# Modulation sums of two feature chunks: from TensorE to VectorE, with the other sums of the stage at new places

## The chip, the core and the metric

The kernel runs on one core of one Trainium2 chip. The metric is device time in microseconds (us) of one execution; a run's number is the median of three. The core's engines are TensorE (PE; its weight loads appear as PEld), VectorE (DVE), ScalarE (ACT), GpSimd (POOL) and SyncE (SP, which here only issues DMAs). Each works through its own queue in order and waits on semaphores for the others.

## What is computed

Two encoder layers over a sequence of 256 rows and 1024 features. What matters here is that the modulation of layer l depends on the vector c alone, so that it can be computed at any time before that layer starts:

```python
c_act = silu(c)
for l in range(2):
    shift, scale, gate = split(c_act @ w_ada[l] + b_ada[l], 3)
    h = rms_norm(x, pre_norm_g[l]) * (1 + scale) + shift
    proj = h @ w_in[l]            # q k v g_att | u b c g_conv
    att = dilated_attention(q, k, v, rel_bias) * silu(g_att)
    cnv = b * short_conv(c * u, conv_w[l]) * silu(g_conv)
    x = x + gate * rms_norm(concat(att, cnv) @ w_out[l], post_norm_g[l])
```

## The kernel before

The feature dimension is cut into 8 chunks of 128. Large products are made exact by splitting each fp32 operand into a high part (`hi`, a ScalarE cast) and a rest (`lo`, a VectorE subtraction), and multiplying three times (`mm3`, lines 270 to 272).

**The main stage of the first layer** is a loop over 24 units (j = 0 to 23, line 816): `UNITS` names 12 column blocks (u0 u1 c0 c1 b0 b1 a1 g0 g1 o0 o1 o2), two units each. Units 0 to 17 are projections, 18 to 23 the start of the output product. Around each unit's matmuls stand, in the order of the code: the PE steps of attention, `scores` of head h at unit 2+2h, its `softmax` in the same unit, `divide` a unit later, `turn` (four transposes, line 596) two units later, `take` (every second head) three units later; the split of the weights that are used four units later (`AHEAD`); and the steps that `PLAN` lists for the unit. PE, ACT, DVE and POOL run in exactly the order in which the code is written (`MANUAL`), so `PLAN` is a hand-written schedule. In it `<` steps come before the unit's attention steps, `=` and `+` steps after the split, `>` steps after the matmuls.

**The modulation of the second layer** is made inside this stage, as two columns per chunk, shift and scale. There are two ways:

- *On PE* (`sums`, `cols`; chunks in `MODS_PE`, a pair at a time): `mods_sums` (line 658) multiplies two 1 MB weight blocks by the replicated silu(c), 16 small fp32 matmuls (line 312), ACT copies the result (line 317); a unit later `mods_cols` folds it with two matmuls (line 331) and three tiny DVE instructions (lines 665 to 667).
- *On DVE* (`shift`, `scale`; a chunk at a time): with the block transposed on the host, each is one dot product over the free dimension, 128x1024, with a read of its accumulator (`dot`, line 299). A chunk is two dots and one 1 MB block, named d0 to d5 here.

Before, chunks 4 and 5 (`s2`) and 6 and 7 (`s3`) are made on PE, chunks 0 to 3 (d0 to d3) on DVE. The gate sums r0 and r1 go over PE too.

**Loads.** `LOADS` is the order of SP's queue: 1 MB blocks (`s` and `r` names are two blocks) into a ring of six `raw` buffers. `load_more` issues a block once the one six places ahead of it has been consumed in the code, and on the chip its DMA waits for that reader.

**The end of the stage.** After unit 23 come the last products of the first half of the sequence (o3), their squares (ACT, line 215), the gated product `og` (DVE, line 869), `rstd` (POOL, lines 221 to 227), the new x (DVE, line 874), `xhat` and its transposes on PE (line 894), which feed the second layer.

Of the kernel before, what the change touches and what calls it, by code (L numbers as in the profile page):

```python
# [33 lines left out]


UNITS = ("u0 u1 c0 c1 b0 b1 a1 g0 g1 o0 o1 o2", "q0 k0 q1 k1 u0 u1 c0 c1 b0 b1 a0 a1 g0 g1 o0 o1 o2")
LOADS = ("u1 c0 c1 b0 r0 d0 b1 s2 a1 r1 g0 s3 g1 d1 d2 o0 o1 o2 d3 o3", "q0 k0 q1 k1 u0 u1 e0 c0 c1 e1 b0 b1 a0 a1 g0 g1 o0 o1 o2 o3")
HEAD_AT = ((2, 4, 6, 8, 10, 12, 14, 16), (6, 8, 11, 13, 16, 18, 21, 23))
PLAN = ({-1: "=heads0", 0: "=heads1", 3: "=heads2", 5: "=heads3", 6: "<gate0 +shift0", 7: "+scale0", 8: "<sums2 =taps0 =line0",
# [6 lines left out]
COLS = {"q": 0, "k": AW, "a": 3 * AW, "u": 4 * AW, "b": 4 * AW + CW, "c": 4 * AW + 2 * CW, "g": 4 * AW + 3 * CW}  # L46

ADA_PE = (0, 1)
MODS_PE = (2, 3)
LAST_ORDER = "g v store q0 k0 q1 k1"  # L50
OUT_K = (0, 4, 6, 2)
ROW_ORDER = "q0 q1 sums k0 cols k1 g v"
# [26 lines left out]
def ada_layout(w_ada):  # L79


    def by_input(l, cols):
        return [w_ada[l][:, a:b].reshape(KC, P, b - a).transpose(1, 0, 2).reshape(P, -1) for a, b in cols]

    def by_feature(l, starts):
        return np.concatenate([w_ada[l][:, a:a + P].T for a in starts], axis=1)
# [8 lines left out]
    for s in range(4):  # L95
        a = 2 * s * P
        blocks[1] += (by_input(1, ((a, a + WC), (D + a, D + a + WC))) if s in MODS_PE
                      else [by_feature(1, (a + j * P, D + a + j * P)) for j in range(2)])
# [29 lines left out]
def encoder_kernel(ctx, tc, x, w_ada, b_ada, w_row, w_cols, w_out, post_g, vecs, bias, out):  # L128
# [277 lines left out]
    for l in range(DEPTH):  # L406
# [283 lines left out]
        def load_more():  # L690

            while todo and all(n < 6 or n - 6 in consumed for n in range(len(loaded), len(loaded) + (2 if todo[0][0] in "sr" else 1))):
                load(todo.pop(0))
# [17 lines left out]
        def split_unit(name, m, late=False):  # L711

            if name[0] == "o":
                src, shape = raws[name][:, m, :], [P, D]
            elif (name, m) not in parts_of:
                src, shape = raws[name][:, :, m * P:(m + 1) * P], [P, KC, P]
            else:
                return lambda: None
            hi, lo = parts_of[name, m] = [wp.tile(shape, F32R, name=n, bufs=6) for n in ("hi", "lo")]
            nc.scalar.copy(hi, src)  # L720

            def second():
                nc.vector.tensor_sub(lo, src, hi.bitcast(F32))  # L723
                if m:
                    consumed.update(load_no[name])

            return second if late else second()
# [77 lines left out]
        if l == 0:  # L805
            for m, w in enumerate(w_u):
                parts_of["u0", m] = w
        todo = LOADS[l].split()
        load_more()
        o_ps = None  # L810
        for j in range(AHEAD):
            split_unit(*splits[j])
        for what in PLAN[l].get(-1, "").split():
            does[what[1:-1]](int(what[-1]))
        load_more()
        for j, (name, m) in enumerate(units):
            stage = {j - at: h for h, at in enumerate(HEAD_AT[l])}
            late = PLAN[l].get(j, "").split()
            for what in [w for w in late if w[0] == "<"]:
# [155 lines left out]
```

## Time and profile before

| What | Value |
|---|---|
| median of 3 runs | 293.22 us (293.03 to 293.94) |
| the profiled execution | 293.09 us, span 291.3 us |
| PE busy | 279.3 us, 96% of the span |
| DVE busy | 210.5 us, 72% |
| ACT busy | 176.0 us, 60% |
| granted TensorE clock, mean | 0.993 of full speed |

The span runs from the first to the last instruction; 1.8 us of the execution lie around it. The shares are averages: a stage in which PE never waits and a stage in which it waits for a chain over ACT, DVE and POOL stand in the same number. The main stage of the first layer lies at about 56 to 144 us of the span, the passage to the second layer at 144 to 166 us, the second layer behind it. In a row of the timeline the first number is the start in us, the second the duration in us; brackets give the time that the engine stood idle before the instruction, and who released it. Instructions of one engine overlap a little, so a step is read from start to start.

### The profile page before, as it was taken

The numbers are of one execution on the slowest core, as the hardware profiler recorded it, in microseconds if no ns is written. First come the engines' busy times: TensorE is split into PE (matmuls) and PEld (weight loads), VectorE is DVE, ScalarE is ACT, GpSimd is POOL, SyncE is SP. The second block draws the span as 40 slices with busy tenths as digits, with TensorE's granted clock in tenths as the row PEclk, the third lists the DMA queues.
The fourth block names the chain that finished last, engine by engine and source line by source line (L and its number), as shares of the span: only waits on it lengthen the run. The fifth ranks groups of instructions, "written<-read, shape, count | busy, mean of one in ns | idle before, by whom it ended". The sixth has DMA issues, their size and how long they took to land.

```text
span 291.3 us, 5502 instructions
## 1 busy us (share of the span) xinstructions
PE 279.3 (96%) x2213; PEld 252.7 (87%) x2213; DVE 210.5 (72%) x371; ACT 176.0 (60%) x318; POOL 20.7 (7%) x43
## 2 busy tenths in 40 slices
PE   7999999999999999999999899999999999999991
PEld 5868999999879879987786899999999999998880
DVE  3649999797785767769889895667887865468234
ACT  4556464999746545576366773957856655946121
POOL 2122000000000000000034400000002000000011
PEclk9999999999999999999999999999999999999997
DMA  7999999998499989755754888445477441000012
GB/s 275 415 422 415 412 403 401 414 427 334 142 389 411 378 324 373 255 197 198 281 234 145 339 313 313 168 150 204 168 251 268 150 155 61 2 0 2 1 72 73
DMA packets 12342, 72.35 MB, mean 248 GB/s; under 512 B 1635, under 2 KB 2921, under 8 KB 5020
## 3 DMA queue, kind: packets, MB, share of 16 engines
q1 hardware_dynamic: 11264, 70.39, 62.3%
q0 software_dynamic: 576, 1.09, 1.1%
q10 hardware_dynamic: 476, 0.52, 0.5%
q8 instruction: 17, 0.28, 0.4%
q14 instruction: 9, 0.07, 0.1%
HBM read 70.92 MB, written 1.07 MB: 247 GB/s over the span
## 4 chain that ended last, share of the span: by engine, by line
PE 84%; ACT 6%; DVE 6%; DMA 1%; issue 1%; POOL 1%; DVEq 0%; ACTq 0%; POOLq 0%
PE pm L270 21%; PE pm L271 21%; PE pm L272 21%; PE pm L312 3%; PE ps L604 2%; PE ps L596 2%; DVE lo L723 2%; PE ps L272 2%; PE ps L270 2%; PE ps L271 2%; PE ps L567 2%; DMA vt<-in_vecs 1%; ACT hi L720 1%; PE ps L568 1%; PE ps L414 1%
## 5 line engine op out<-in xcount | busy, mean ns | idle before, releaser
L270 PE MATMUL pm<-hT_hi,hi 128*128 128x256 f32 x408 | 116.1, 284 | 0.8 <-ACT hT_hi L498 0.8
L271 PE MATMUL pm<-hT_lo,hi 128*128 128x256 f32 x408 | 114.0, 279 | 0.1
L272 PE MATMUL pm<-hT_hi,lo 128*128 128x256 f32 x408 | 113.9, 279 | 0.0
L723 DVE TENSOR_TENSOR lo<-raw,hi 128x1024 fp32r<-128x1024 f32 x60 | 72.9, 1223 | 37.4 <-ACT hi L720 37.3
L270 PEld LDWEIGHTS pm<-hT_hi,hi 128*128 128x128 f32 x408 | 76.7, 188 | 3.4 <-issue 2.0
L271 PEld LDWEIGHTS pm<-hT_lo,hi 128*128 128x128 f32 x408 | 76.8, 188 | 0.5 <-DVE hT_lo L500 0.3
L272 PEld LDWEIGHTS pm<-hT_hi,lo 128*128 128x128 f32 x408 | 76.7, 188 | 0.0
L720 ACT CAST hi<-raw 128x1024 fp32r<-128x1024 f32 x60 | 62.3, 1048 | 5.0 <-PE pm L271 4.7
L443 DVE TENSOR_TENSOR lo<-raw,hi 128x1024 fp32r<-128x1024 f32 (+1 forms) x16 | 17.4, 1087 | 1.4 <-ACT hi L441 1.4
L270 PE MATMUL pm<-hi,hT_hi 128*128 128x256 f32 (+1 forms) x50 | 16.9, 337 | 0.5 <-DVE hT_hi L263 0.5
L580 ACT ACTIVATE prob<-prob,mx 128x256 f32<-128x256 f32 x32 | 16.0, 504 | 2.1 <-DVE mx L577 2.0
L271 PE MATMUL pm<-lo,hT_hi 128*128 128x256 f32 (+1 forms) x50 | 16.7, 334 | 0.6 <-DVE lo L723 0.6
L598 ACT COPY pT<-ps 128x512 f32<-128x512 f32 x16 | 9.4, 587 | 12.2 <-PE ps L596 12.2
L272 PE MATMUL pm<-hi,hT_lo 128*128 128x256 f32 (+1 forms) x50 | 16.7, 334 | 0.0
L577 DVE CUSTOM_DVE_ANT_0 prob<-ps,u 128x256 f32<-128x256 f32 x32 | 12.2, 420 | 5.5 <-PE ps L568 5.3
L589 ACT ACTIVATE prob<-prob,rc 128x256 f32<-128x256 f32 x16 | 8.2, 512 | 12.9 <-DVE rc L587 12.9
L441 ACT CAST hi<-raw 128x1024 fp32r<-128x1024 f32 (+1 forms) x16 | 14.3, 938 | 1.7 <-DMA raw<-in_w_row 1.7
L215 ACT ACTIVATE junk<-pm 128x512 f32<-128x512 f32 (+1 forms) x9 | 5.0, 550 | 16.6 <-PE pm L272 9.6
L299 DVE CUSTOM_DVE_ANT_0 raw<-raw,c_row,scale_g 128x1024 f32<-128x1024 f32 x10 | 13.4, 1342 | 0.0
L270 PE MATMUL pm<-hi,mix_a 128*128 128x512 f32 (+1 forms) x36 | 13.3, 370 | 0.0
L271 PE MATMUL pm<-lo,mix_a 128*128 128x512 f32 (+1 forms) x36 | 13.3, 370 | 0.0
L272 PE MATMUL pm<-hi,mix_a 128*128 128x512 f32 (+1 forms) x36 | 13.3, 370 | 0.0
(185 smaller groups left out, 473.3 us busy)
## 6 DMA issues: line engine op xcount, KB each, us to landing
raw<-in_w_cols SPq DMA_DIRECT2D x25, 1024.0 KB, 6.6
raw<-in_w_ada SPq DMA_DIRECT2D x24, 1024.0 KB, 8.0
raw<-in_w_out SPq DMA_DIRECT2D x8, 1024.0 KB, 4.8
raw<-in_w_row SPq DMA_DIRECT2D x7, 896.0 KB, 7.5
u<-t_dr SPq DMA_DIRECT2D x1, 1536.0 KB, 11.0
x_sb<-in_x SPq DMA_DIRECT2D x2, 512.0 KB, 4.5
gg<-r_dr POOLq DMA_DIRECT2D x2, 512.0 KB, 4.7
raw<-in_w_row SPq DMA_DIRECT2D x1, 512.0 KB, 7.8
```

Source lines behind the costliest of these rows:

```text
L270: nc.tensor.matmul(o, ah, bh, start=first, stop=False, **kw)
L271: nc.tensor.matmul(o, ah, bl, start=False, stop=False, **kw)
L272: return nc.tensor.matmul(o, al, bh, start=False, stop=last, **kw)
L299: nc.vector.tensor_tensor_reduce(w, w, c_row, scale=factor, scalar=first, op0=ALU.mult, op1=ALU.add, accum_out=o)
L312: nc.tensor.matmul(g_ps[32 * j:32 * j + 32, :], c_rep[:, kk + kh * (KC // 2), :], raws[t][:, kk + kh * (KC // 2), :], start=kk == 0, stop= ...
L441: nc.scalar.copy(hi, src)
L443: nc.vector.tensor_sub(lo, src, hi.bitcast(F32))
L577: nc.vector.tensor_tensor_reduce(pr_sb[:, t, :], s_ps[:, t, :], u[:, h, t * P:t * P + S][:, ::-1], scale=-1.0, scalar=3.0e38, op0=ALU.add, ...
L580: nc.scalar.activation(pr_sb[:, t, :], pr_sb[:, t, :], AF.Exp, scale=-1.0, bias=mx[:, t:t + 1], accum_out=sm[:, t:t + 1])
L598: nc.scalar.copy(pT[h], t_ps)
L720: nc.scalar.copy(hi, src)
L723: nc.vector.tensor_sub(lo, src, hi.bitcast(F32))
```

## The change

Chunks 4 and 5 leave `MODS_PE`. Their two weight blocks, of the same size, are laid out by feature, and become d4 and d5. In `PLAN` of the first layer `sums2` and `cols2` are gone, and four dots come in; nearly all dots stand at other units:

| Chunk | Before: shift, scale at unit | After |
|---|---|---|
| 0 | 6, 7 | 2, 4 |
| 4 | on PE: sums 8, cols 9 | 6, 7 |
| 1 | 13, 14 | 13, 14 |
| 2 | 16, 19 | 15, 16 |
| 5 | on PE, with 4 | 19, 21 |
| 3 | 20, 21 | 22, 23 |

`LOADS` follows: d0 goes from behind r0 to ahead of b0, d4 and d5 stand where they are needed, d3 comes last. The second layer's plan is the same.

```diff
-LOADS = ("u1 c0 c1 b0 r0 d0 b1 s2 a1 r1 g0 s3 g1 d1 d2 o0 o1 o2 d3 o3", ...
+LOADS = ("u1 c0 c1 d0 b0 r0 b1 d4 a1 r1 g0 s3 g1 d1 d2 o0 o1 o2 d5 o3 d3", ...
...
-         15: "+early0", 16: "+shift2", 17: "+side1 +sg0 >sg1 >turn0 >turn1", 18: "=conv0 =whole0", 19: "=conv1 +scale2", 20: "=att1 +shift3", 21: "+scale3"},
+         15: "+early0 +shift2", 16: "+scale2", 17: "+side1 +sg0 >sg1 >turn0 >turn1", 18: "=conv0 =whole0", 19: "=conv1 +shift5",
+         20: "=att1", 21: "+scale5", 22: "+shift3", 23: "+scale3"},
...
-MODS_PE = (2, 3)
+MODS_PE = (3,)
```

The file has one line more, so line numbers of after are higher by one. In the rows below a dot is two rows, one that reads a `raw` tile and `c_row`, and one that reads the accumulator into a column of B (shift) or A (scale).

DVE in units 2 and 3, before: the rest of a weight split, then the divide of head 0 (`rc`, `prob`).

```order
L723 TENSOR_TENSOR lo_809<-raw_715,hi_808 128x1024
L587 RECIPROCAL rc_844<-sm_813 128x2
L588 TENSOR_SCALAR prob_811<-prob_811,rc_844 128x256
L723 TENSOR_TENSOR lo_849<-raw_715,hi_848 128x1024
L399 SCALAR_TENSOR_TENSOR q_even_663<-pm_233,q_even_663 64x512
```

And after:

```order
L724 TENSOR_TENSOR lo_809<-raw_715,hi_808 128x1024
L300 ISA raw_717,B1_112<-raw_717,c_row_105,vt_89 128x1024
L300 ISA B1_112 128x1
L588 RECIPROCAL rc_845<-sm_813 128x2
L589 TENSOR_SCALAR prob_811<-prob_811,rc_845 128x256
L724 TENSOR_TENSOR lo_850<-raw_715,hi_849 128x1024
L400 SCALAR_TENSOR_TENSOR q_even_663<-pm_233,q_even_663 64x512
```

The shift dot of chunk 0 now stands ahead of the divide of head 0.

DVE in units 15 and 16, before: the gated first half of attention (`att`, `att_a`), then the softmax of the last head.

```order
L723 TENSOR_TENSOR lo_1510<-raw_1302,hi_1509 128x1024
L646 TENSOR_TENSOR att_666<-att_666,sg0_242 128x512
L648 TENSOR_TENSOR att_a_1513<-att_666,att_a_1513 128x512
L577 ISA prob_1556,mx_1557<-ps_1541,u_106 128x256
L577 ISA mx_1557 128x1
```

And after:

```order
L724 TENSOR_TENSOR lo_1485<-raw_1277,hi_1484 128x1024
L647 TENSOR_TENSOR att_666<-att_666,sg0_242 128x512
L649 TENSOR_TENSOR att_a_1488<-att_666,att_a_1488 128x512
L300 ISA raw_1233,B1_112<-raw_1233,c_row_105,vt_89 128x1024
L300 ISA B1_112 128x1
L578 ISA prob_1532,mx_1533<-ps_1517,u_106 128x256
L578 ISA mx_1533 128x1
```

The shift dot of chunk 2 now stands ahead of that softmax; its scale dot takes the old place of the shift dot, behind the softmax and the next split.

DVE from unit 20 on, before: the two splits of o3, the second half of attention, two dots of chunk 3, the first gated product.

```order
L723 TENSOR_TENSOR lo_1686<-raw_1472,hi_1685 128x1024
L646 TENSOR_TENSOR att_666<-att_666,sga_1598 128x512
L648 TENSOR_TENSOR hT_lo_108<-att_666,hT_hi_107 128x512
L299 ISA raw_1422,B1_112<-raw_1422,c_row_105,vt_89 128x1024
L299 ISA B1_112 128x1
L723 TENSOR_TENSOR lo_1700<-raw_1472,hi_1699 128x1024
L299 ISA raw_1422,A1_111<-raw_1422,c_row_105,scale_g_103,vt_89 128x1024
L299 ISA A1_111 128x1
L869 TENSOR_TENSOR og_1730<-pm_1644,gg_1642 128x512
```

And after:

```order
L724 TENSOR_TENSOR lo_1664<-raw_1447,hi_1663 128x1024
L647 TENSOR_TENSOR att_666<-att_666,sga_1576 128x512
L649 TENSOR_TENSOR hT_lo_108<-att_666,hT_hi_107 128x512
L724 TENSOR_TENSOR lo_1677<-raw_1447,hi_1676 128x1024
L300 ISA raw_1397,A1_111<-raw_1397,c_row_105,scale_g_103,vt_89 128x1024
L300 ISA A1_111 128x1
L300 ISA raw_1541,B1_112<-raw_1541,c_row_105,vt_89 128x1024
L300 ISA B1_112 128x1
L300 ISA raw_1541,A1_111<-raw_1541,c_row_105,scale_g_103,vt_89 128x1024
L300 ISA A1_111 128x1
L870 TENSOR_TENSOR og_1709<-pm_1622,gg_1620 128x512
```

No dot stands between the two splits of o3 any more; three stand behind them, directly ahead of the first gated product.

## Rows read from the trace of the kernel before

**Rows 1.** Page, part 4: the chain that ended last, shares by engine.

```profile
PE 84%; ACT 6%; DVE 6%; DMA 1%; issue 1%; POOL 1%; DVEq 0%; ACTq 0%; POOLq 0%
```

**Rows 2.** Busy time in three stretches; columns are named in the first row.

```profile
core 0: us, PE busy (x) PEld busy (x) DVE busy (x) ACT busy (x) POOL busy (x), PEclk, DMA share, GB/s
53.10:69.20 16.10, 16.10 (x135) 15.87 (x134) 13.29 (x21) 15.25 (x25) 0.00 (x0) 1.00 1.01 419
69.20:85.10 15.90, 15.90 (x152) 14.04 (x150) 12.30 (x24) 12.03 (x24) 0.00 (x0) 1.00 0.67 255
...
127.90:143.10 15.20, 14.23 (x66) 10.37 (x64) 12.17 (x16) 9.53 (x14) 0.00 (x0) 1.00 0.56 208
```

**Rows 3.** PE in order of time, around sums and columns: start, duration, instruction.

```profile
84.77 0.28 PE L271 MATMUL pm<-hT_lo,hi 128*128 128x256 f32 x1
84.89 0.27 PE L272 MATMUL pm<-hT_hi,lo 128*128 128x256 f32 x1
85.09 1.93 PE L312 MATMUL pm<-raw,c_rep 128*32 128x256 f32 x32
...
87.18 0.28 PE L568 MATMUL ps<-k_low,q_odd 128*128 128x256 f32 x1
...
90.67 0.28 PE L272 MATMUL pm<-hT_hi,lo 128*128 128x256 f32 x1
...
91.36 0.28 PE L271 MATMUL pm<-hT_lo,hi 128*128 128x256 f32 x1
```

**Rows 4.** DVE in order of time, late in the main stage (two dots).

```profile
125.53 1.28 DVE L299 CUSTOM_DVE_ANT_0 raw<-raw,c_row,vt 128x1024 f32<-128x1024 f32 x1
...
126.73 0.16 DVE L587 RECIPROCAL rc<-sm 128x2 f32<-128x2 f32 x1
...
136.19 1.34 DVE L299 CUSTOM_DVE_ANT_0 raw<-raw,c_row,scale_g 128x1024 f32<-128x1024 f32 x1
...
137.46 1.22 DVE L723 TENSOR_TENSOR lo<-raw,hi 128x1024 fp32r<-128x1024 f32 x1
```

**Rows 5.** ACT's share of the divide of heads 0 and 1, in order of time.

```profile
67.23 0.52 ACT L589 ACTIVATE prob<-prob,rc 128x256 f32<-128x256 f32 x1 [0.46 <-DVE rc L587]
...
73.70 0.51 ACT L589 ACTIVATE prob<-prob,rc 128x256 f32<-128x256 f32 x1 [0.38 <-DVE rc L587]
```

**Rows 6.** PE in order of time: the turns of heads 0 and 1.

```profile
69.17 0.60 PE L596 MATMUL ps<-ident,prob 128*128 128x128 f32 x4
...
77.75 0.60 PE L596 MATMUL ps<-ident,prob 128*128 128x128 f32 x4
```

**Rows 7.** SP's issue of b0, and DMA issues there: KB, us to landing.

```profile
50.33 0.33 SPq L197 DMA_DIRECT2D raw<-in_w_cols  x1
...
raw<-in_w_cols SPq DMA_DIRECT2D x1, 1024.0 KB, 11.6
```

**Rows 8.** DVE in order of time: first softmax instruction of head 5, unit 12.

```profile
107.39 0.42 DVE L577 CUSTOM_DVE_ANT_0 prob<-ps,u 128x256 f32<-128x256 f32 x1 [0.31 <-PE ps L568]
```

**Rows 9.** DVE in order of time: the end of the output sums, first half.

```profile
144.60 0.69 DVE L869 TENSOR_TENSOR og<-pm,gg 128x512 f32<-128x512 f32 x1 [0.28 <-ACT junk L215]
...
146.00 0.69 DVE L869 TENSOR_TENSOR og<-pm,gg 128x512 f32<-128x512 f32 x1 [0.71 <-ACT junk L215]
146.99 1.42 DVE L874 SCALAR_TENSOR_TENSOR x_sb<-og,rstd,x_sb 128x512 f32<-128x512 f32 x2 [0.30 <-POOL rstd L227]
```

**Rows 10.** PE in order of time: three waits after unit 17.

```profile
130.33 0.50 PE L270 MATMUL pm<-hi,att_a 128*128 128x512 f32 x1 [0.42 <-ACT sga L638]
...
143.11 0.50 PE L271 MATMUL pm<-lo,hT_hi 128*128 128x512 f32 x1 [0.56 <-DVE lo L723]
...
161.32 0.85 PE L894 MATMUL ps<-ident,xhat 128*128 128x128 f32 x6 [1.10 <-DVE xhat L928]
```

**Rows 11.** POOL in order of time: the same instruction twice.

```profile
144.75 0.23 POOL L221 TENSOR_SCALAR ms_eps<-ms 128x1 f32<-128x1 f32 x1 [21.36 <-ACT junk L215]
...
153.15 1.10 POOL L221 TENSOR_SCALAR ms_eps<-ms 128x1 f32<-128x1 f32 x1 [2.04 <-ACT junk L215]
```

More of the change, by code (lines that the diff above doesn't have):

```diff
@@ L36 @@
 UNITS = ("u0 u1 c0 c1 b0 b1 a1 g0 g1 o0 o1 o2", "q0 k0 q1 k1 u0 u1 c0 c1 b0 b1 a0 a1 g0 g1 o0 o1 o2")
-LOADS = ("u1 c0 c1 b0 r0 d0 b1 s2 a1 r1 g0 s3 g1 d1 d2 o0 o1 o2 d3 o3", "q0 k0 q1 k1 u0 u1 e0 c0 c1 e1 b0 b1 a0 a1 g0 g1 o0 o1 o2 o3")
+LOADS = ("u1 c0 c1 d0 b0 r0 b1 d4 a1 r1 g0 s3 g1 d1 d2 o0 o1 o2 d5 o3 d3", "q0 k0 q1 k1 u0 u1 e0 c0 c1 e1 b0 b1 a0 a1 g0 g1 o0 o1 o2 o3")
 HEAD_AT = ((2, 4, 6, 8, 10, 12, 14, 16), (6, 8, 11, 13, 16, 18, 21, 23))
-PLAN = ({-1: "=heads0", 0: "=heads1", 3: "=heads2", 5: "=heads3", 6: "<gate0 +shift0", 7: "+scale0", 8: "<sums2 =taps0 =line0",
[2 rows of a table removed]
+PLAN = ({-1: "=heads0", 0: "=heads1", 2: "+shift0", 3: "=heads2", 4: "+scale0", 5: "=heads3", 6: "<gate0 +shift4", 7: "+scale4",
[3 rows of a table added]
         {1: "=store0", 4: "=heads0", 5: "=heads1 =line0", 7: "+dot0", 8: "+dot1", 9: "=heads2", 10: "=heads3", 11: "+dot2", 12: "+dot3",
```

2 rows, old and new, of the table PLAN are left out of this document.

## The prediction

> **What bounds the kernel now.** I read the chain of waits first: PE holds 84% of it [rows 1]. So PE time counts wherever PE is not waiting, and the question is where that holds. The busy times by stretch tell it: from 53 to 85 us PE is busy all the time, while ACT is busy 15.25 of 16.10 us in the first half of this and DVE 13.29 [rows 2]. There is little room on those two at the start of the stage. From 128 to 143 us PE has about a microsecond of idle time in 15.2 [rows 2], and the timeline names three waits: for ACT's `sga` at 130.33, for a DVE split at 143.11, and for DVE's `xhat` at 161.32 [rows 10]. So the main stage is bound by PE up to about unit 17; from there to the second layer, chains over ACT and DVE end last at three places, and the last of them hands its delay to all that follows.
>
> **What is removed.** One `sums` and one `cols` on PE, both in the stretch where PE never waits. With the sums, PE needs 87.18 − 84.89 = 2.29 us from the last projection matmul of unit 7 to the second score matmul of unit 8; an ordinary step is 84.89 − 84.77 = 0.12 us, so two ordinary steps would be 0.24 and the sums cost 2.05 us [rows 3]. (The bar of 1.93 us is less, because the neighbours are slowed at both ends.) In the same way the columns cost 91.36 − 90.67 − 0.24 = 0.45 us [rows 3]. Together PE gains **2.50 us**. The ACT copy and the three tiny DVE instructions also go; they lie beside PE's projections of units 8 and 9, and I count nothing for them; were ACT or DVE what PE waits for there, they would be a further gain.
>
> **What is added.** Four dots on DVE. From the start of a shift dot to the next instruction it is 126.73 − 125.53 = 1.20 us, for a scale dot 137.46 − 136.19 = 1.27 us [rows 4]. So 4.94 us in all. Where they stand decides what they cost.
>
> *The early pair (units 2 and 4).* The dot at unit 2 stands ahead of the divide of head 0. ACT's half of the divide began at 67.23 and takes 0.51 [rows 5]; 1.20 later it ends at 68.94. PE turns this head at 69.17 [rows 6]: 0.23 us are left. The scale dot at unit 4 adds 1.27 to the divide of head 1: 73.70 + 2.47 + 0.51 = 76.68, against the turn at 77.75 [rows 5, 6], 1.07 us left. Units 6 and 7 hold two dots before and after. So DVE and ACT run up to 2.5 us late here, but PE should not wait. From unit 8 on PE is 2.5 us earlier itself, and the lag must be made up: DVE has room from here on, 12.30 us busy of 15.90 [rows 2], and at unit 12 it waited for PE's scores, 0.31 us [rows 8]. I take it that the lag has gone by then. Cost: nothing, as long as the 0.23 us hold.
>
> *The late pair.* Counted from unit 15 to the first `og`, before has two shift and two scale dots, after three of each: 1.20 + 1.27 = 2.47 us more, all ahead of the first gated product. The dot ahead of the last softmax delays the divide, `sga`, and so the wait at 130.33 by about 1.2 us; that spends half of the gain for a while. But chunk 3's shift dot no longer stands ahead of the split that PE waits for at 143.11 [rows 10], so PE gets about all of its lead back there, and this place does not set the end. The end of the stage does. There DVE now has three dots in a row, while PE's last products are done 2.5 us sooner. Idle time that can take the dots up is what DVE spends waiting there for ACT's squares and POOL's `rstd`: 0.28 + 0.71 + 0.30 = 1.29 us [rows 9]. So the new x is written 2.47 − 1.29 = **1.18 us later** than DVE would with the full lead. From it come `rstd`, `xhat` and the transposes at 161.32, for which PE already waits [rows 10]: the 1.18 goes through to the second layer, where PE is busy throughout and nothing gives it back.
>
> *The moved loads.* d0 takes b0's place in SP's queue, issued at 50.33, and a block takes 11.6 us to land there [rows 7]: 61.9, five microseconds ahead of its dot at about 67. b0 moves one place back, and is split only at unit 4. d4 and d5 are as large as the blocks of `s2`. d3 is loaded last, and its ring place is freed by the scale dot at unit 23; the load that waits for that is a block of the second layer. I count nothing for the loads; if d0 came late after all, the dot would wait at the head of DVE's queue, with the divide of head 0 and so PE's turn behind it.
>
> **Sum.** 2.50 − 1.18 = 1.32 us. The profiled execution took 293.09 us, so the same execution would be 291.8; against the median of 293.22, which is 0.13 above it, **291.9 us**.
>
> **Rivals.**
>
> *DVE does not bind at the end.* If the squares and `rstd` come late enough anyway, or DVE recovers between the two halves, all of the 2.50 stays: 290.7. For it speaks that DVE idles in this stretch, 12.17 us busy of 15.20 [rows 2]; against it, that the dots stand behind the last split, where only 1.29 us of idle time is left [rows 9]. 12%.
>
> *POOL is held up.* The same tiny POOL instruction took 0.23 us at 144.75 and 1.10 at 153.15 [rows 11]; at the second place DVE was subtracting two SBUF tensors. The dots also read two SBUF tensors, and now run just when POOL makes `rstd`, in three instructions. One held instruction costs 0.87, which hides behind DVE's own 1.18; two cost 1.74, of which 0.56 shows: 2.50 − 1.74 = 0.76 gained, 292.5. The Trainium skill states the rule in "SBUF — State Buffer", section "SBUF: two separate sides": VectorE and GpSimd share a port pair that is held for a whole instruction, by a VectorE instruction with two SBUF inputs against a GpSimd one that reads SBUF. By that rule this trace's 1.10 us is a blocked instruction, and the three dots speak against the change at this one place. 10%.
>
> *Nothing left.* If the squares and `rstd` move with the dots, so that the idle 1.29 us takes up nothing, 2.47 of 2.50 is lost: 293.2. 10%.
>
> *The early pair starves PE.* ACT is 95% busy up to 69 us [rows 2] and works in turns with DVE, so a dot between divide and split may delay both. If the 0.23 us at unit 2 don't hold and no idle time takes up the two dots, PE waits 2.47 us in units 4 to 8: 2.50 − 2.47 − 1.18 = −1.15, **slower**, 294.4. It is slower by more than can be told once 2.2 of the 2.47 us reach PE. Against it: PE must first use up the 1.07 us at unit 6 [rows 5, 6]. 6%.
>
> **How the numbers follow.** My forecast gets the remaining 62%, with its own range of 291.3 to 292.5. A measurement of this kernel can tell about 0.3% from no change, 0.88 us, so faster means below 292.34. Most of the forecast's share (about 56 of 62) and the first rival are faster: 0.68. What is left of the forecast, the held POOL and "nothing left" are within 0.3%: 0.26. Slower is the starved start: 0.06. The range of 290.7 to 292.9 leaves out "nothing left" and the slower case, 16%, and a little at the edges.
>
> **What the changed profile would show.** The fp32 matmuls of line 313 onto `pm` are 32 records fewer [rows 3], and PE runs from unit 7's last projection to the scores in ordinary steps. The turns of heads 0 and 1 start where they did, with no PE wait: if not, the early pair costs. At unit 12 DVE still waits for PE's scores, 2.5 us sooner. The wait for `sga` grows by about a microsecond; the one for the last split of o3 nearly goes. Three dots stand directly ahead of the first `og`, DVE no longer waits for ACT's squares there, and PE waits longer for both `xhat`, about 1.2 us more in all. The second layer, from its first split to the last output, is as long as before; if it is not, something I have not counted moved there. The forecast is wrong if `og` starts earlier than about 0.2 us before its old time (more gain), or if `rstd` and not DVE ends last (less).

## The result, and the profile after

| | before | after |
|---|---|---|
| median | 293.55 us (293.03 to 293.94, 4 runs) | 291.77 us (291.39 to 291.93, 4 runs) |
| the profiled execution | 293.09 us, span 291.3 | 291.87 us, span 290.2 |

The ratio is 0.9938, with a 95% interval of 0.9911 to 0.9964: faster by about 0.6%. Line numbers of after are higher by one. In its page, first the busy times, then the chain of work that ended last by engine and by line, against [rows 1]:

```profile
PE 277.7 (96%) x2177; PEld 251.6 (87%) x2177; DVE 214.4 (74%) x376; ACT 175.8 (61%) x317; POOL 21.3 (7%) x43
...
PE 80%; DVE 9%; ACT 5%; issue 2%; DMA 1%; POOL 1%; DVEq 0%; ACTq 0%; POOLq 0%
PE pm L271 20%; PE pm L272 20%; PE pm L273 20%; DVE raw L300 3%; PE ps L605 2%; PE ps L597 2%; PE pm L313 2%; PE ps L271 2%; PE ps L273 2%; PE ps L272 2%; PE ps L568 2%; DVE lo L724 2%; DMA vt<-in_vecs 1%; ACT hi L721 1%; PE ps L569 1%
```

The dots, line 300, are now 3% of the chain: somewhere a dot ends last. The timeline of DVE at the end of the stage says where, against [rows 9]:

```profile
139.97 1.23 DVE L724 TENSOR_TENSOR lo<-raw,hi 128x1024 fp32r<-128x1024 f32 x1 [0.26 <-ACT hi L721]
141.11 1.34 DVE L300 CUSTOM_DVE_ANT_0 raw<-raw,c_row,scale_g 128x1024 f32<-128x1024 f32 x1
...
142.37 1.28 DVE L300 CUSTOM_DVE_ANT_0 raw<-raw,c_row,vt 128x1024 f32<-128x1024 f32 x1
...
143.58 1.34 DVE L300 CUSTOM_DVE_ANT_0 raw<-raw,c_row,scale_g 128x1024 f32<-128x1024 f32 x1
...
144.85 1.28 DVE L870 TENSOR_TENSOR og<-pm,gg 128x512 f32<-128x512 f32 x2
146.05 1.41 DVE L875 SCALAR_TENSOR_TENSOR x_sb<-og,rstd,x_sb 128x512 f32<-128x512 f32 x2
```

Three dots stand in a row ahead of `og`, and from the last split to the new x there is no bracket: the 0.28, 0.71 and 0.30 us of [rows 9] are gone, and DVE ends last. What PE waited for between 50 and 168 us (total, times, longest), against [rows 10]:

```profile
PE pm L271 <- ACT sga L639: 0.9, 1, 0.9
PE ps L895 <- DVE xhat L929: 0.9, 1, 0.9
PE pm L271 <- DVE hT_hi L264: 0.6, 1, 0.6
PE ps L895 <- DVE xhat L913: 0.5, 1, 0.5
PE ps L597 <- DVE prob L589: 0.5, 1, 0.5
```

The wait for the last split of o3 is gone; the turn of head 7 (line 597) and the first `xhat` are new waits.

**A measure that leaves the start out.** The first microseconds of the kernel differ by up to 2.4 us between the profiled executions (last section). So the stage is taken by itself: from the first matmul of the r0 sums on PE (line 312 of before) to the second `xhat` on DVE. In all kernels below it is followed by 130.8 to 131.0 us to the end of the span, so all that the changes did lies in it or ahead of it.

| Kernel | median us | ratio to before, 95% | r0 sums at | first x at | second xhat at | stage |
|---|---|---|---|---|---|---|
| before | 293.55 | | 75.30 | 146.99 | 160.42 | 85.12 |
| after | 291.77 | 0.9938 (0.9911 to 0.9964) | 75.79 | 146.05 | 159.25 | 83.46 |
| a2_again | 291.68 | 0.9948 (0.9932 to 0.9965) | 75.28 | 145.57 | 158.77 | 83.49 |
| q1_no_sums | 290.20 | 0.9901 (0.9888 to 0.9913) | 75.13 | 144.30 | 157.51 | 82.38 |
| p1_last_dot_out | 291.55 | 0.9951 (0.9930 to 0.9971) | 77.31 | 146.75 | 159.97 | 82.66 |
| n0_no_d0 | 291.87 | 0.9957 (0.9945 to 0.9969) | 75.73 | 146.03 | 159.23 | 83.50 |
| t1_twice | 292.36 | 0.9972 (0.9956 to 0.9987) | 76.40 | 146.68 | 159.88 | 83.48 |
| s1_ahead_of_split | 292.86 | 0.9999 (0.9977 to 1.0022) | 75.31 | 146.81 | 160.03 | 84.72 |
| g1_gaps | 291.03 | 0.9930 (0.9916 to 0.9943) | 75.72 | 145.31 | 158.53 | 82.81 |
| g2_gaps | 289.62 | 0.9875 (0.9862 to 0.9889) | 75.97 | 144.29 | 157.51 | 81.54 |
| m2_places_only | 292.31 | 0.9971 (0.9951 to 0.9992) | 77.55 | 148.38 | 161.81 | 84.26 |
| h1_all_dots | 288.35 | 0.9826 (0.9804 to 0.9849) | 75.39 | 142.19 | 155.40 | 80.01 |

The medians of before beside the experiments were 293.09 to 293.45 us. The last four columns are of one profiled execution each.

### The profile page after: what moved, and what is told of

It is laid out like the page before. It is cut to its first block, busy times and chain, and to the rows that moved or that the text cites. A ratio compares the mean times of both kernels' runs of the same rounds, so it can differ in the third digit from the quotient of the medians.

```text
span 290.2 us, 5435 instructions
## 1 busy us (share of the span) xinstructions
PE 277.7 (96%) x2177; PEld 251.6 (87%) x2177; DVE 214.4 (74%) x376; ACT 175.8 (61%) x317; POOL 21.3 (7%) x43
## 3 DMA queue, kind: packets, MB, share of 16 engines
q0 software_dynamic: 576, 1.09, 1.2%
## 4 chain that ended last, share of the span: by engine, by line
PE 80%; DVE 9%; ACT 5%; issue 2%; DMA 1%; POOL 1%; DVEq 0%; ACTq 0%; POOLq 0%
PE pm L271 20%; PE pm L272 20%; PE pm L273 20%; DVE raw L300 3%; PE ps L605 2%; PE ps L597 2%; PE pm L313 2%; PE ps L271 2%; PE ps L273 2%; PE ps L272 2%; PE ps L568 2%; DVE lo L724 2%; DMA vt<-in_vecs 1%; ACT hi L721 1%; PE ps L569 1%
## 5 line engine op out<-in xcount | busy, mean ns | idle before, releaser
L300 DVE CUSTOM_DVE_ANT_0 raw<-raw,c_row,scale_g 128x1024 f32<-128x1024 f32 x12 | 16.1, 1342 | 0.0
L300 DVE CUSTOM_DVE_ANT_0 raw<-raw,c_row,vt 128x1024 f32<-128x1024 f32 x12 | 15.4, 1280 | 0.0
L271 PE MATMUL pm<-hi,mix_a 128*128 128x512 f32 (+1 forms) x36 | 13.3, 371 | 0.0
```

The costliest lines, as they stand in the source:

```text
L271: nc.tensor.matmul(o, ah, bh, start=first, stop=False, **kw)
L300: nc.vector.tensor_tensor_reduce(w, w, c_row, scale=factor, scalar=first, op0=ALU.mult, op1=ALU.add, accum_out=o)
```

## The experiments

My theory was that of the prediction: PE gains 2.5 us, and the late dots give about half of it back because they stand ahead of the first gated product. The rival was that the missing gain went elsewhere: at the early pair, over POOL, or that only the number of dots counts and not their place.

**What PE gains with nothing added.** `q1_no_sums`, from before:

```diff
-            cv["acc"] = sums([of_inputs(raw, WC)[0] for raw in raws[f"s{s}"]], pm, "pm")
+            if s != 2:
+                cv["acc"] = sums([of_inputs(raw, WC)[0] for raw in raws[f"s{s}"]], pm, "pm")
...
+            if s == 2:
+                nc.vector.tensor_copy(B[:, ks], vt[:, c0:c0 + 2])
+                nc.vector.tensor_copy(A[:, ks], scale1[:, l + 1, ks])
+            else:
+                col_ps = columns(cv["acc"], pm, "pm")
...
```

> The kernel before, with the sums and columns of chunks 4 and 5 left out on PE and nothing put in their place (these two chunks' shift and scale columns are not computed; loads and all other steps as before). My theory: PE gains 2.05 + 0.45 = 2.50 us from unit 8 on, and with no dot added DVE follows with its whole lead, so that the stage ends 2.3 to 2.5 us sooner: 293.55 - 2.4 = 291.1 (ratio 0.991 to 0.992). Rival, that the chains over ACT and DVE at the end of the stage hold it anyway: under 1.3 us, no better than the changed kernel at 291.8.

DVE at the end of the stage:

```profile
140.28 1.34 DVE L299 CUSTOM_DVE_ANT_0 raw<-raw,c_row,scale_g 128x1024 f32<-128x1024 f32 x1
...
141.91 0.69 DVE L874 TENSOR_TENSOR og<-pm,gg 128x512 f32<-128x512 f32 x1 [0.28 <-ACT junk L215]
143.31 0.69 DVE L874 TENSOR_TENSOR og<-pm,gg 128x512 f32<-128x512 f32 x1 [0.71 <-ACT junk L215]
144.30 1.42 DVE L879 SCALAR_TENSOR_TENSOR x_sb<-og,rstd,x_sb 128x512 f32<-128x512 f32 x2 [0.30 <-POOL rstd L227]
```

From the r0 sums, `og` comes at 141.91 - 75.13 = 66.78 against 144.60 - 75.30 = 69.30 before: 2.52 us sooner, with the waits of before word for word. The whole lead of PE reaches x; another 0.22 us comes behind it. The stage is 2.74 us shorter. The rival, under 1.3 us, has fallen.

**The late dots.** `p1_last_dot_out`, from after; `noscale` copies a constant into the column in place of the dot:

```diff
-         20: "=att1", 21: "+scale5", 22: "+shift3", 23: "+scale3"},
+         20: "=att1", 21: "+scale5", 22: "+shift3", 23: "+noscale3"},
```

> The changed kernel with the last of the three late dots left out (chunk 3's scale column is not computed). My theory, that the dots ahead of the first gated product end last there: DVE comes 1.27 us sooner to the gated product, but then rstd ends last; it was ready at about 145.6 against x at 146.05, and with no dot beside POOL's three instructions it may come at 145.2 (as far behind the squares as before): x is 0.4 to 0.85 us sooner, and so the end: 290.9 to 291.4 (ratio 0.991 to 0.993). Rival, that the gain that is missing was lost elsewhere: as the changed kernel, 291.8. Rival, that DVE alone binds: 1.27 us, 290.5.

The first x comes at 69.44 us from the r0 sums against 70.26 in after, 0.82 sooner, and the stage is 0.80 shorter, near the upper end of what was expected. The median, 291.55, is above the 290.9 to 291.4 expected. The start of the profiled execution was 2.05 us later than before (last section); whether the others started late too is not shown, as only one execution of each kernel has a trace. The gain is less than the dot's 1.27 because another chain now ends last, as DVE's row of x shows:

```profile
145.20 1.28 DVE L874 TENSOR_TENSOR og<-pm,gg 128x512 f32<-128x512 f32 x2
146.75 1.41 DVE L879 SCALAR_TENSOR_TENSOR x_sb<-og,rstd,x_sb 128x512 f32<-128x512 f32 x2 [0.27 <-POOL rstd L228]
```

The three instructions of POOL that make this `rstd`, first in after, where dots run beside the first two, then here, where the last dot ends at 145.2:

```profile
142.95 0.79 POOL L222 TENSOR_SCALAR ms_eps<-ms 128x1 f32<-128x1 f32 x1 [21.64 <-ACT junk L216]
144.33 0.65 POOL L225 TENSOR_TENSOR me<-ms_eps,ms 128x1 f32<-128x1 f32 x1 [0.59 <-ACT junk L216]
145.05 0.57 POOL L228 TENSOR_TENSOR rstd<-me,neg_half 128x1 f32<-128x1 f32 x1
```

```profile
144.50 0.80 POOL L222 TENSOR_SCALAR ms_eps<-ms 128x1 f32<-128x1 f32 x1 [21.64 <-ACT junk L216]
145.88 0.19 POOL L225 TENSOR_TENSOR me<-ms_eps,ms 128x1 f32<-128x1 f32 x1 [0.58 <-ACT junk L216]
146.15 0.57 POOL L228 TENSOR_TENSOR rstd<-me,neg_half 128x1 f32<-128x1 f32 x1
```

In after both long ones end within 0.16 us of the step from a dot to the next instruction of DVE (143.74 and 144.98, against 143.58 and 144.85). In the second kernel only the first has a dot beside it, and only it is long; with none beside them, as in q1_no_sums, they take 0.23 and 0.19 us. The rival of the prediction was real: two instructions held, 0.56 + 0.46 = 1.02 us. But `rstd` was ready at 145.62 and DVE came to x at 146.05, so it cost nothing. The two held instructions agree with the Trainium skill, "SBUF — State Buffer", section "SBUF: two separate sides": a VectorE instruction with two SBUF inputs and a GpSimd instruction that reads SBUF lock each other out of a shared port pair for a whole instruction.

**Place or number?** `s1_ahead_of_split`, from after:

```diff
-         15: "+early0 +shift2", 16: "+scale2", 17: "+side1 +sg0 >sg1 >turn0 >turn1", 18: "=conv0 =whole0", 19: "=conv1 +shift5",
-         20: "=att1", 21: "+scale5", 22: "+shift3", 23: "+scale3"},
+         15: "+early0 +shift2", 16: "+scale2", 17: "+side1 +sg0 >sg1 >turn0 >turn1", 18: "=conv0 =whole0 +shift5", 19: "=conv1 +scale5",
+         20: "=att1 +shift3", 21: "+scale3"},
```

> The changed kernel with its last four dots two units sooner (shift 5, scale 5, shift 3, scale 3 at units 18, 19, 20, 21): the same number of dots, three instead of one of them ahead of the last split of o3, one instead of three behind it. My theory, that what ends last at a place counts and not the number of dots: PE waits for the split, which starts at about 142.2 instead of 139.97; the gated product follows a split by 2.77 us where PE is between them, so it starts at 145.0 and its second half at 146.4, x at 147.4 instead of 146.05. The stage is 1.3 us longer than that of the changed kernel, 84.8 against 83.46; 293.1 in all. Rival, that only the number of dots ahead of the gated product counts: 83.46 and 291.8.

PE at the last split of o3:

```profile
142.92 0.50 PE L272 MATMUL pm<-lo,hT_hi 128*128 128x512 f32 x1 [1.61 <-DVE lo L724]
```

The first x came at 71.50 us from the r0 sums (expected 71.6), the stage is 84.72 (84.8): the same work in another order leaves 0.40 us of the 1.66. In the runs no gain can be told (ratio 0.9977 to 1.0022). The rival, the number of dots, has fallen.

**The early pair.** `n0_no_d0` puts copies of constants in the place of the dots of units 2 and 4; `t1_twice` makes the dot of unit 2 twice:

```diff
-            shift_of(l + 1, k, raws[f"d{k}"])
+            for _ in range(2 if (l, k) == (0, 0) else 1):
+                shift_of(l + 1, k, raws[f"d{k}"])
```

> The changed kernel with the early pair left out (chunk 0's shift and scale columns are not computed). My theory, that the early pair is hidden but for the 0.1 us that PE waits at the turn of head 0: 0 to 0.15 us sooner, 291.6 to 291.8. Rival, that the pair delays the splits and heads of the stage's start beyond its cover: 0.5 us or more sooner, 291.3 or less.

> The changed kernel with the dot of unit 2 made twice (chunk 0's shift column is not the reference's). From the first transposes on PE to the first of the r0 sums: before 66.20 us, changed 66.31, early pair left out 66.15. My theory, that the cover of the dot at unit 2 is used up to the last 0.2 us, so that any further time there is PE's: the second dot makes PE wait 1.1 to 1.2 us at the turn of head 0, this stretch is 67.3 to 67.5 us, and the rest, from the r0 sums to the second xhat, stays 83.46; 292.9 in all. Rival, that PE or the end of the stage takes it up: 291.8.

Without the pair the stage is 83.50 and the median 291.87: nothing gained. From the first transposes on PE (9.12 us in a2_again) to the r0 sums it takes 66.15 without the pair, 66.16 with it in a2_again, and 66.31 in the first profiled run of after, where ACT waited 0.37 us longer than before for a weight block. So the pair costs 0.01 us, and 0.16 where that block came late. ACT's row with that wait, before, in after and in a2_again:

```profile
52.04 2.00 ACT L191 CAST hi<-raw 128x1024 fp32r<-128x1024 f32 x2 [0.67 <-DMA raw<-in_w_cols]
```

```profile
52.79 2.00 ACT L192 CAST hi<-raw 128x1024 fp32r<-128x1024 f32 x2 [1.04 <-DMA raw<-in_w_cols]
```

```profile
51.75 2.00 ACT L192 CAST hi<-raw 128x1024 fp32r<-128x1024 f32 x2 [0.36 <-DMA raw<-in_w_cols]
```

With the dot made twice the stretch is 66.77, 0.61 more than in a2_again and not the 1.1 to 1.2 expected. The two halves of the divide and PE at the turn of head 0:

```profile
69.79 0.51 ACT L590 ACTIVATE prob<-prob,rc 128x256 f32<-128x256 f32 x1 [3.00 <-DVE rc L588]
69.79 0.35 DVE L589 TENSOR_SCALAR prob<-prob,rc 128x256 f32<-128x256 f32 x1
...
70.20 0.66 PE L597 MATMUL ps<-ident,prob 128*128 128x128 f32 x4 [0.35 <-DVE prob L589]
```

The first two transposes read the half that DVE divides. So PE turns 0.41 us after the start of the halves, 0.06 behind the end of DVE's, and not after the end of ACT's (0.51). In a2_again the halves start at 68.14 and PE turns at 69.15: a slack of 0.60 us and not 0.23. In the first profiled run of after they start at 69.18 and PE turns at 69.59, 0.41 behind: there the late block left no slack. The rest of my claim stood: what PE loses at unit 2 is not made up, the stage from the r0 sums is 83.48.

**Dots into DVE's own waits.** The timeline of DVE in after shows a wait for ACT's cast in every odd unit from 3 to 17, between the divide and the next split:

```profile
94.06 1.23 DVE L724 TENSOR_TENSOR lo<-raw,hi 128x1024 fp32r<-128x1024 f32 x1 [1.18 <-ACT hi L721]
...
101.56 1.23 DVE L724 TENSOR_TENSOR lo<-raw,hi 128x1024 fp32r<-128x1024 f32 x1 [1.18 <-ACT hi L721]
...
110.14 1.22 DVE L724 TENSOR_TENSOR lo<-raw,hi 128x1024 fp32r<-128x1024 f32 x1 [1.13 <-ACT hi L721]
...
118.37 1.23 DVE L724 TENSOR_TENSOR lo<-raw,hi 128x1024 fp32r<-128x1024 f32 x1 [1.13 <-ACT hi L721]
```

A dot takes 1.20 to 1.27. `g1_gaps` gives `PLAN` a fourth kind of step, `~`, made directly ahead of the split, and uses it:

```diff
+            for what in [w for w in late if w[0] == "~"]:
+                does[what[1:-1]](int(what[-1]))
             if second:
                 second()
...
+PLAN = ({-1: "=heads0", 0: "=heads1", 3: "~shift0 =heads2", 5: "~scale0 =heads3", 6: "<gate0 +shift4", 7: "~scale4",
+         8: "=taps0 =line0", 9: "=taps1", 10: "<gate1 =taps2", 11: "=taps3", 12: "<rows0 <sums3", 13: "~shift1 =cols3", 14: "+scale1",
+         15: "~shift2 +early0", 16: "+scale2", 17: "~shift5 +side1 +sg0 >sg1 >turn0 >turn1", 18: "=scale5 =conv0 =whole0", 19: "=conv1 +shift3",
+         20: "=att1", 21: "+scale3"},
```

> The changed kernel with its dots at other places: in an odd unit DVE waits about 1.13 us for ACT's cast between the divide and the next split, as long as a dot; shift 0, scale 0, scale 4, shift 1, shift 2 and shift 5 go there (units 3, 5, 7, 13, 15, 17), scale 5 goes ahead of the convolution's products in unit 18, chunk 3's dots to units 19 and 21. One dot instead of three stands between the last split of o3 and the first gated product. My theory: DVE no longer ends last there, rstd does, and the waits of PE for the turn of head 7 and for sga (0.47 and 0.88 us) fall by about a dot, so squares come sooner too: 0.8 to 1.6 us sooner than the changed kernel, 290.2 to 291.0. Rival, that only the number of dots counts and not where they stand: 291.8. Rival, that the gap dots hold up the splits that PE needs: 292 or more.

The stage fell to 82.81, 0.65 less than after; I had expected 0.8 to 1.6. The squares came no sooner, because PE had a wait in place of the others:

```profile
141.43 0.50 PE L272 MATMUL pm<-lo,hT_hi 128*128 128x512 f32 x1 [0.75 <-DVE lo L724]
```

`scale5` in unit 18 stands on the way to that split. So `g2_gaps`:

```diff
+         8: "=taps0 =line0", 9: "=taps1", 10: "<gate1 =taps2", 11: "=taps3", 12: "<rows0 <sums3", 13: "~shift1 =cols3", 14: "~scale1",
+         15: "~shift2 +early0", 16: "+scale2", 17: "~shift5 +scale5 +side1 +sg0 >sg1 >turn0 >turn1", 18: "=conv0 =whole0", 19: "=conv1 +shift3",
```

> As the kernel with dots in the gaps, with scale 5 moved into DVE's wait for ACT's silu (unit 17, ahead of the gated convolution) and scale 1 into its wait for the cast in unit 14. There PE still waited 0.75 us for the last split of o3, because a dot stood ahead of it. Length of the stage, from the first of the r0 sums on PE to the second xhat on DVE: before 85.12, changed kernel 83.46, gaps 82.81, PE sums left out 82.38. My theory, that a dot costs nothing in a DVE wait of its length and its full time ahead of the last split: the wait for that split goes, and the stage is as short as with no dots added, 82.3 to 82.6; 290.3 to 290.7 in all. Rival, that the wait only moves on to another dot or to ACT: 82.8 or more.

PE's waits between 50 and 168 us are now three:

```profile
PE ps L897 <- DVE xhat L931: 0.9, 1, 0.9
PE pm L271 <- DVE hT_hi L264: 0.5, 1, 0.5
PE pm L271 <- ACT sga L639: 0.4, 1, 0.4
```

The stage is 81.54 us, shorter than expected (82.3 to 82.6). My floor was wrong: q1_no_sums adds no dot but keeps the places of before, with its wait of 0.57 us for the last split. With 289.62 us, ratio 0.9875 (0.9862 to 0.9889), this beats both kernels.

**The places without the swap.** `m2_places_only` is before with `~shift1` in unit 13, `~scale1` in 14, and

```diff
-         15: "+early0", 16: "+shift2", 17: "+side1 +sg0 >sg1 >turn0 >turn1", 18: "=conv0 =whole0", 19: "=conv1 +scale2", 20: "=att1 +shift3", 21: "+scale3"},
+         15: "~shift2 +early0", 16: "+scale2", 17: "+side1 +sg0 >sg1 >turn0 >turn1", 18: "=conv0 =whole0", 19: "=conv1 +shift3", 20: "=att1", 21: "+scale3"},
```

> The kernel before, its sums of chunks 4 and 5 still on PE, with the dots of chunks 1 to 3 alone moved into DVE's waits: shift 1, scale 1, shift 2 ahead of the splits of units 13 to 15, scale 2 from unit 19 to 16, shift 3 from 20 to 19. My theory, that places and the swap are two gains that add up: PE's wait of 0.56 us for the last split of o3 goes, and the stage from the first of the r0 sums to the second xhat falls from 85.12 to 84.0 - 84.4; 292.1 to 292.5 in all. With the swap on top the second version with gaps measured 81.54, so the swap would be worth 2.5 to 2.9 us where its dots stand in waits. Rival, that the places help only because of the swap: 85.1, 293.4.

The stage is 84.26, as expected: 0.86 us shorter from places alone, ratio 0.9971 (0.9951 to 0.9992). From there to g2_gaps the swap is worth 84.26 - 81.54 = 2.72 us, all that q1_no_sums showed (2.74). With the places that after gives its dots, swap and places together are worth 1.66.

**The same swap once more.** `h1_all_dots` takes chunks 6 and 7 off PE too:

```diff
-MODS_PE = (3,)
+MODS_PE = ()
...
+         8: "=taps0 =line0", 9: "=taps1", 10: "<gate1 ~shift6 =taps2", 11: "~scale6 =taps3", 12: "<rows0 ~shift7", 13: "~scale7", 14: "~shift1",
+         15: "~scale1 ~shift2 +early0", 16: "+scale2", 17: "~shift5 +scale5 +side1 +sg0 >sg1 >turn0 >turn1", 18: "=conv0 =whole0", 19: "=conv1 +shift3",
```

> The second version with gaps, with the last pair on PE (chunks 6 and 7) made by dots as well: shift 6, scale 6, shift 7, scale 7 ahead of the splits of units 10 to 13, shift 1 in 14, scale 1 and shift 2 in 15. PE loses another 2.5 us of sums; DVE had 7.4 us of waits between 91 and 122 us, and takes 4.94 more of dots while the stretch gets 2.5 us shorter. Theory, that a dot in a wait is free: the stage falls from 81.54 to 79.0 - 79.6, 287.1 to 287.7 in all. Rival, that the waits are now full and DVE binds from unit 13 on: 80.5 to 81.5, 288.6 to 289.6. Rival, that DVE falls so far behind that PE waits more than the sums cost: over 81.6.

The stage is 80.01 us, 1.53 less than in g2_gaps: between the two cases. 288.35 us, ratio 0.9826 (0.9804 to 0.9849), is the best kernel here. The swap freed less of PE than the 2.5 us expected. The scores of head 6 (unit 14), in g2_gaps, then here:

```profile
111.81 0.28 PE L568 MATMUL ps<-k_hh,q_even 128*128 128x256 f32 x1
```

```profile
109.06 0.28 PE L568 MATMUL ps<-k_hh,q_even 128*128 128x256 f32 x1
```

From the r0 sums that is 35.84 and 33.67 us: PE is 2.17 us ahead, and 0.64 of it is gone by the second `xhat`. Of DVE's rows from 90 to 119 us, those with a wait and the dots at the end of this stretch:

```profile
91.82 1.23 DVE L724 TENSOR_TENSOR lo<-raw,hi 128x1024 fp32r<-128x1024 f32 x1 [1.18 <-ACT hi L721]
...
111.14 1.28 DVE L300 CUSTOM_DVE_ANT_0 raw<-raw,c_row,vt 128x1024 f32<-128x1024 f32 x1
...
113.94 1.34 DVE L300 CUSTOM_DVE_ANT_0 raw<-raw,c_row,scale_g 128x1024 f32<-128x1024 f32 x1
115.20 1.28 DVE L300 CUSTOM_DVE_ANT_0 raw<-raw,c_row,vt 128x1024 f32<-128x1024 f32 x1
...
118.92 0.69 DVE L649 TENSOR_TENSOR att_a<-att,att_a 128x512 fp32r<-128x512 f32 x1 [0.69 <-ACT att_a L648]
```

DVE has no wait of more than 0.11 us between 91.82 and 118.92; PE's wait for `sga` behind it is 0.89 us, against 0.42 in g2_gaps, which is 0.47 of the 0.64. The waits are full.

**After once more.** `a2_again` is the changed kernel, unchanged, on the same chip as g2_gaps, s1_ahead_of_split and t1_twice.

> The changed kernel once more, on the same chip as the experiments. Both theories: 291.4 to 292.0, the stage from the r0 sums to the second xhat 83.4 to 83.5 us, three dots ahead of the first gated product. What is open is the start of the kernel: PE's 16 matmuls that make c_rep's row took 2.02 us before and 2.32 in the changed kernel, 0.38 us later in all. If that goes with the program, it is there again; if it is chance, it is not, and the run is 0.4 us faster.

Stage 83.49, as expected, and the start was 0.36 us earlier than in the first profiled run: the late start does not go with the program.

## Why the prediction was right, and where it was not

- **The bound.** PE in the stage, chains over ACT and DVE at its end: right. q1_no_sums shows that the 2.5 us of PE taken away at units 8 and 9 reach the end in full.
- **PE's gain, 2.50 us.** Measured 2.52 (q1_no_sums). Start to start, not bar to bar, was the right reading of [rows 3]. Counting nothing for the ACT copy was right. The tiny DVE instructions are not tested: q1_no_sums still has three.
- **The early pair, nothing.** Right but for 0.01 to 0.16 us. The step that was mis-sized is the time from the divide to the turn: PE waits for DVE's half, and turns 0.41 us behind the start of the halves, not 0.51. The slack was not a fixed 0.23 us either. From the first transposes the halves started 0.89 us later than before in a2_again (68.14 - 9.12 = 59.02 against 67.23 - 9.10 = 58.13), where ACT waited 0.31 less for the weight block, and 1.57 later in the first profiled run of after, where it waited 0.37 more: 1.20 for the dot both times, as counted, with 0.60 and 0.00 us of slack.
- **The lag is made up by unit 12.** The first softmax of unit 12 still came at 106.10, only 1.29 us before [rows 8] and without waiting for PE; the split behind it waited 0.47 us for ACT and stood 2.07 us earlier, as PE did. Gone within that unit.
- **The late pair, 1.18 us.** Against q1_no_sums, where nothing is added, `og` came 69.06 - 66.78 = 2.28 us later and x 70.26 - 69.17 = 1.09, where 1.18 were forecast: of the 2.47 us of dots 1.38 were taken up by waits, where 1.29 were counted. The mechanism is shown by p1_last_dot_out and s1_ahead_of_split.
- **The moved loads, nothing.** No run moves them alone. The swap is worth 2.72 us with the new order of loads (m2_places_only against g2_gaps) and 2.74 with the old one (q1_no_sums), and the stretch ahead of the r0 sums is 66.20 us before and 66.16 in a2_again. Both speak for nothing.
- **PE's waits.** The wait for `sga` grew from 0.42 to 0.88 us, by 0.46 where about 1 was forecast; the one for the last split went. PE's waits in all grew from 2.58 us (0.42, 0.56, 0.50 for the first `hT_hi`, 1.10) to 3.36 (0.47, 0.88, 0.55, 0.58, 0.88), by 0.78 and not 1.2; of it only 0.33 stands at the two `xhat`, because 0.47 is at the turn of head 7, which I had not named: the dot ahead of the last softmax delays that turn before it delays `sga`.
- **The sum, 1.32 us.** The stage shows 85.12 - 83.46 = 1.66. The difference: 0.09 at the late pair, 0.02 at PE, and 0.23 between the first x and the second `xhat`, which took 13.43 us before and 13.20 after. I had not counted this. It is 13.43 in the two profiles of kernels with the sums of chunks 4 and 5 on PE (before, m2_places_only), where POOL's line 224 began 1.49 us behind the end of its line 221 and `rstd` ended last for the second x; it is 13.20 to 13.22 in all others, and in q1_no_sums, whose waits are otherwise those of before, POOL's gap is 1.20. It begins at ACT's second squares, which wait 0.44 us for PE before and 0.16 in q1_no_sums, while PE's rows stand at the same distance from the first x. What links this to the sums is open.
- **The time, 291.9 us.** That it came so near to 291.77 is partly luck. It was counted from a median of 293.22, and beside the result before took 293.55: the medians gained 1.78 us, not 1.32. The profiled executions gained 1.22, because the r0 sums stood 0.49 us later in that of after, which hides the 0.34 that the stage gained beyond the sum.
- **The rivals.** POOL was held up as described, by 1.02 us and not 1.74, and was hidden. The starved start came only with the dot made twice. "DVE does not bind" is ruled out by p1_last_dot_out, "nothing left" by the stage: x came 1.09 us later than in q1_no_sums, not 2.47.

## What to carry to other kernels

Work moved to an engine that is less busy is paid at the place where it stands in that engine's queue: the same dots made the stage 0.40, 1.66 or 3.58 us shorter by their order alone. Look for the waits of the receiving engine that recur and are as long as the moved piece, and put it directly ahead of the instruction that waits; then look which wait ends last, and move the piece that stands on the way to it. Stop when the receiving engine's waits are full: the second swap still gained, but lost 0.64 of its 2.17 us.

## What was not expected of the hardware

The start of the kernel is not the same in every run. PE's first rows, of a2_again, then of m2_places_only:

```profile
1.30 3.46 PE L415 MATMUL ps<-zeros 128*128 128x256 f32 x8 [1.30 <-DVE zeros L163]
5.53 2.02 PE L454 MATMUL ps<-ident,c_rep 128*128 128x128 f32 x16 [0.77 <-ACT c_rep L449]
7.39 1.89 PE L415 MATMUL ps<-zeros 128*128 128x256 f32 x8
```

```profile
1.30 3.78 PE L414 MATMUL ps<-zeros 128*128 128x256 f32 x8 [1.30 <-DVE zeros L162]
5.96 3.75 PE L453 MATMUL ps<-ident,c_rep 128*128 128x128 f32 x16 [0.87 <-ACT c_rep L448]
9.50 2.06 PE L414 MATMUL ps<-zeros 128*128 128x256 f32 x8
```

Eight matmuls take 3.46 us first and 1.89 later in a2_again, 3.78 and 2.06 in m2_places_only. The granted clock in the rows is 1.00 of full speed all this time, so it does not show a reason, and the cause is open. The sixteen that follow took 2.02 us in five of the profiled kernels, 2.32 to 2.70 in five, and 3.75 or 3.76 in two, and what follows comes later by about as much: the first transposes stood at 8.97 to 11.40 us. It happened with the code of before and of after alike. The spread of a kernel's runs (290.41 to 293.62 us for p1_last_dot_out) is larger than that; how much of it is the start is not shown. A comparison of two single profiles has to leave this start out.
